# Weight splits handed out earlier in some stretches, and a scan column cleared through its table: a two-layer decoder trunk on one core

## The chip, the cores and the metric

The kernel runs on one core of a Trainium2 chip. The metric is the device time of one execution in microseconds (us), the median over runs. The engines are PE (TensorE: matmuls and transposes), DVE (VectorE), ACT (ScalarE), POOL (GpSimd) and SP (SyncE, which here only issues the loads of weights). Each engine works through its own list of instructions in order; semaphores between the lists keep the data dependences.

## The reference

Two layers on a sequence of 256 positions of width 1024, batch 1, all in float32:

```python
for l in range(DEPTH):                       # DEPTH = 2
    h = h + 0.5 * swiglu(rms_norm(h, ffn1_norm[l]), ...)            # 1024 -> 2816 -> 1024
    h = h + hybrid_mixer(rms_norm(h, mix_norm[l]), w_in[l], ...)    # S5 scan | differential attention
    h = h + memory_cross_attention(rms_norm(h, xattn_norm[l]), rms_norm(mem, mem_norm[l]), ...)
    h = h + 0.5 * swiglu(rms_norm(h, ffn2_norm[l]), ...)
return rms_norm(h, final_norm)
```

The mixer projects its input by `w_in` (1024 to 2048) into the input of a state-space scan (32 groups of 64 complex states, `lax.associative_scan` over the 256 positions) and the q, k, v of a causal differential attention with 4 heads. The scan's result goes through a gelu and a gated projection (`w_glu`, `glu` below). Both halves are normalised, concatenated and projected by `w_out`. The cross-attention reads 256 memory tokens by `wkv` (keys and values).

## The kernel before

*Weights and splits.* All weights are read once, as 512 KB units that SP loads into one of four buffers `raw`. A matmul of float32 accuracy is made of three reduced-precision ones (`fp32r`): a weight is split into a high half `whi` (ACT, with a copy that rounds) and a low half `wlo` (DVE, `raw` less `whi`, scaled by the norm's gain where there is one), the activations into `xh` and `xl` in the same way; PE then does `whi*xh`, `wlo*xh`, `whi*xl`, a triplet of 128x512 matmuls. A unit is split in two steps (q = 0, 1), each one instruction on ACT and one on DVE. Five pairs of `whi` and `wlo` (N_W) are held. In the second feed-forward a unit is split whole, 128x1024 at once. In `wkv` the moving operand is the memory, named `mem`; in the down projections and `w_glu` it is named `gT` or `yT`.

*What sets the order.* The kernel is written out by a planner in Python, which keeps a rough clock for each engine. `stream_plan` (L104) lists all weight units in the order in which PE uses them, and beside it `need`, the planned time of each (2 x STEP = 2.56 units of planned time for an ordinary unit). Before PE's matmuls of a unit are written, `feed` (L503) hands out splits, so that they come next in ACT's and DVE's lists: as long as a buffer is free (N_W) and the split's need is no further off than `LEAD` = 4.0 from where PE's main line is planned to be:

```python
if u >= self.nfree + N_W or (u > least and self.need[u] + q * STEP / 2 > self.main + LEAD):
    break
```

All the other work (evacuation of accumulators, normalisation, softmax, the scan) are tasks, Python generators, which the planner resumes as their planned inputs are due; each resumed step appends its instructions to the engines' lists behind the splits handed out so far. So a longer lead puts more splits ahead of the next step of a task on ACT and DVE, and may change when the planner writes a task's transposes into PE's list. `aside()` writes instructions without advancing the task's planned time.

*First feed-forward (ffn1).* For each of 11 chunks of 256 hidden columns and each half t = 0, 1 of the positions: gate and up matmuls into `mm`; ACT's `sg` (the gate's activation), DVE's `g` (the gated product), PE's transposes `tp<-ident,g`, then `gT` (ACT and DVE); the down matmuls into `acc` follow two chunks later. The second feed-forward (ffn2) has the same steps by way of `z` and combined blocks of weights.

*Mixer.* The projection `w_in` comes in four chunks, then `wkv` in three, so that scan and attention can work meanwhile. The scan's input goes out to DRAM and back (`z` to `uq`), is rearranged by ACT (`up`) and transposed by PE (`tp<-ident,up`) to `U`. 64 small matmuls give the inputs to the states in `acc` (pairs 0, 1 real and 2, 3 imaginary), and DVE then does, for each layer:
- rotations `p<-acc,rot` by a table `rot` (`cs_t` in the code: cosine and sine of each state's phase within a segment of 64 columns, made once in each layer by ACT's Sin),
- two scans `p<-dt,p` over 1023 columns, whose decay table `dt` is zero at the end of each segment,
- rotations back by the same table (`p<-p,rot`, 128x1023), and sums.

Each scan's column 0 of every segment of 64 must be zero: two memsets of 128x16. Attention's scores stand in `sb` (with `bias`), their row maxima in `nm`, the q and k transposes in `qkT`.

*Lines.* In the profile all of DVE's work has line L269, ACT's L306, POOL's L329, PE's matmuls L345 and transposes L356, since helpers record them; tiles are told apart by their names. In the changed kernel these lines are 7 further on.

Of the kernel before, what the change touches and what calls it, by code (L numbers as in the profile page):

```python
# [33 lines left out]
N_W = 5  # L34
N_S4 = 12
N_T5 = 3
LEAD = 4.0
STEP = 1.28
MARGIN = 0.2
BURST = 0.8  # L40
# [63 lines left out]
def stream_plan():  # L104

    plan = []
# [44 lines left out]
    need, at, i = [], 0.0, 0  # L151
    while i < len(plan):
        n = plan[i][5]
        need += [at + STEP * k for k in range(n)]
        at += STEP if plan[i][3] == "S" else 2 * STEP * n
        i += n
    return plan, need


class Task:  # L160


    def __init__(self, gen, now):
        self.gen, self.t, self.done, self.waiters = gen, now, False, []
        self.pe = -1.0
# [195 lines left out]
class Trunk:  # L361
    def __init__(self, ctx, tc, io):
        self.tc, self.io = tc, io
        self.c = Clock(tc.nc)
        self.v, self.a, self.g, self.p = Vector(self.c), Scalar(self.c), Pool(self.c), Tensor(self.c)
        P = lambda name, bufs, **kw: ctx.enter_context(tc.tile_pool(name=name, bufs=bufs, **kw))
        self.const = P("const", 1)
        self.xp = P("xp", 2)
        self.rawp = P("raw", N_RAW)
        self.hip = P("hi", N_W)  # L370
        self.lop = P("lo", N_W)
        self.tab = P("tab", 1)
        self.s4 = P("s4", N_S4)
        self.zp = P("zp", 4)
        self.gp = P("gp", 2)
        self.tp5 = P("tp5", N_T5)
        self.jp = P("jp", 1)
        self.sm = P("sm", 4)
        self.sp1 = P("sp1", 1)
        self.acc = P("acc", 4, space=bass.MemoryType.PSUM)  # L380
        self.mm = P("mm", 2, space=bass.MemoryType.PSUM)
        self.tp = P("tp", 1, space=bass.MemoryType.PSUM)
        self.dram = P("dram", 1, space=bass.MemoryType.DRAM)
        self.plan, self.need = stream_plan()
        self.main = 0.0
        self.upos = self.nload = self.nsplit = self.nfree = 0
        self.raw, self.w, self.blk = {}, {}, {}
        self.added, self.content = set(), {}
        self.stream = Task(None, 0.0)
        self.nacc = self.nmm = 0  # L390
        self.accfree = [0.0, 0.0]
        self.mmfree = [0.0, 0.0]
        self.tpfree, self.tpown = [0.0, 0.0], {}
# [109 lines left out]
    def feed(self, least=-1):  # L503

        c = self.c
        prev, c.cur = c.cur, self.stream
        n = len(self.plan)
        while self.nsplit < 2 * n:
            u, q = divmod(self.nsplit, 2)
            if u >= self.nfree + N_W or (u > least and self.need[u] + q * STEP / 2 > self.main + LEAD):  # L510
                break
            self.split_next(self.plan[u][0].startswith("ffn2"))
        c.cur = prev
# [104 lines left out]
    def tick(self, ready):  # L618
        self.feed()
        self.c.run_due()  # L620
        self.c.now = max(self.c.now, ready + 0.13)
        self.main += STEP / 2

# [57 lines left out]
    def opening(self, evac):  # L681
# [12 lines left out]
        def mm(t, k):  # L694
            u, q = divmod(k, 2)
            self.main += STEP / 2
            self.mm_half(ps[t], self.x[t], self.w[u], 2 * u, q, k == 0, False)
# [21 lines left out]
        self.split_next()  # L719
        self.main += STEP  # L720
        wh, wl = (a[:, 0:512] for a in self.w[0][:2])
# [423 lines left out]
    def ssm_tables(self, l, tb):  # L1145
        v, a, g, io = self.v, self.a, self.g, self.io
# [13 lines left out]
        p = self.sp1.tile([128, 3, 16], F32, tag="sp", name="sp")  # L1160
# [12 lines left out]
        dt, mag, th, n, fr, x1, x2 = (t16(k) for k in ("dt", "mag", "th", "n", "fr", "x1", "x2"))  # L1173
# [24 lines left out]
        cs_t = self.tab.tile([128, 2, 1024], F32, tag="tC", name="rot")  # L1198
# [19 lines left out]
        a.activation(cs, x1, AF.Sin, bias=self.halfpi, scale=-1.0)  # L1218
        a.activation(cs_t[:, 1, :], an, AF.Sin, scale=6.283185)
        a.activation(cs_t[:, 0, :], rn, AF.Sin, bias=self.halfpi, scale=-6.283185)  # L1220
        yield

        pw = self.sp1.tile([128, 2, 16, 5], F32, tag="pw", name="pw")
# [43 lines left out]
        for q in range(4):  # L1267
            yield from self.tp_wait()
            ps = self.tpt()
            for i in range(8):  # L1270
                m, ri = 4 * q + i // 2, i % 2
# [24 lines left out]
        for q in range(2):  # L1296
            yield from self.tp_wait()
            ps = self.tpt()
            for i in range(8):
                m = 8 * q + i  # L1300
                if i == 4:
                    yield self.c.now + GAP
                for e in range(2):
                    s = slice(64 * e, 64 * e + 64)
                    o = ps[64 * e:64 * e + 16, 64 * i:64 * i + 64]
# [23 lines left out]
    def mixer(self, l, preps, tb, tables, tail):  # L1329
        v, c = self.v, self.c  # L1330
# [42 lines left out]
        def ssm_states(z_tasks):  # L1373
# [11 lines left out]
            for b in range(2):  # L1385
                yield from self.tp_wait()
                p = self.transpose4(upf, [512 * b + 128 * k for k in range(4)])
# [5 lines left out]
            for ri in range(2):  # L1393
                for gh in range(2):
                    yield c.now + GAP
                    for pp in range(8):
                        m = 8 * gh + pp
# [24 lines left out]
            n = 1023  # L1422
# [3 lines left out]
            y_r = p2  # L1426
            for o, x in ((y_r, p1), (y_i, p3)):
                v.tensor_tensor_scan(o[:, 1:1024], Dk[:, 0:n], x[:, 0:n], 0.0, ALU.mult, ALU.add)
                v.memset(o.rearrange("p (m c) -> p m c", c=64)[:, :, 0], 0.0)
            yield  # L1430
            xr, xi = p1, y_r
            v.memset(xr[:, 0:1], 0.0)
            s1 = slice(1, 1024)
            tt(xr[:, s1], y_r[:, s1], C[:, 0:n], ALU.mult)
            tt(p3[:, s1], y_i[:, s1], S[:, 0:n], ALU.mult)
# [179 lines left out]
        self.kT = []  # L1615
        zt = self.project("w_in", self.x, ssm_evac, preps)
        states = c.spawn(ssm_states(zt))
        qt = self.project("w_in", self.x, qk_evac(0))
        kt = self.project("w_in", self.x, qk_evac(1))
        vk = []  # L1620
        at = [c.spawn(attn(t, qt + kt, vk)) for t in range(2)]
# [323 lines left out]
```

## Time and profile before

| | |
|---|---|
| median of 3 runs | 1203.88 us (1203.52 to 1204.22) |
| the profiled execution | 1203.8 us |
| its span, first to last instruction | 1201.1 us |
| mean granted clock of PE | 0.998 |
| busy: PE, DVE, ACT, POOL | 1187.6, 903.0, 711.9, 45.3 us |
| mean rate of the HBM | 173 GB/s |

2.7 us of the profiled execution lie around its span. Matmuls are pipelined: a row of PE gives the time of one from its start to its modelled end (0.39 us), while the next one starts 0.23 us after it. "idle before" in square brackets is what an engine stood still ahead of a row, and what ended that.

### The profile page before, as it was taken

How to read it: one execution, taken by the hardware profiler on the slowest of the kernel's cores; microseconds unless marked ns; L12 is line 12 of the kernel's file. 1: busy time of each engine (PE TensorE's matmuls, PEld its weight loads, DVE VectorE, ACT ScalarE, POOL GpSimd, SP SyncE). 2: the span in 40 equal slices, each digit the busy share in tenths (PEclk: the TensorE clock that was granted, in tenths of full speed). 3: DMA queues.
4: the chain of work that ended last, by engine and by line, in shares of the span. 5: the costliest groups of instructions: out<-in, count | busy, mean ns of one | idle time of the engine just before them, and what ended most of it. 6: DMA issues, size and time to landing. Idle time of an engine off the chain costs nothing.

```text
span 1201.1 us, 17736 instructions
## 1 busy us (share of the span) xinstructions
PE 1187.6 (99%) x6583; PEld 971.6 (81%) x6583; DVE 903.0 (75%) x1498; ACT 711.9 (59%) x1206; POOL 45.3 (4%) x104
## 2 busy tenths in 40 slices
PE   9999999999999999999999999999999999999997
PEld 7888888777888888888888888888678888888886
DVE  5797776498866688978668879565978675889785
ACT  6665455556856566555465545555687665666553
POOL 2100001000000000000010000100000000000000
PEclk9999999999999999999999999999999999999999
DMA  8656556534644466374565655654436455746542
GB/s 281 212 182 198 161 172 173 173 124 139 193 159 141 156 219 221 128 263 135 176 194 181 192 171 175 186 168 150 140 121 197 158 158 169 294 133 215 191 140 86
DMA packets 59974, 210.91 MB, mean 176 GB/s; under 512 B 7168, under 2 KB 8288, under 8 KB 59888
## 3 DMA queue, kind: packets, MB, share of 16 engines
q1 hardware_dynamic: 56304, 202.92, 52.5%
q0 software_dynamic: 2000, 5.24, 1.5%
q10 hardware_dynamic: 1584, 1.62, 0.5%
q8 instruction: 51, 0.84, 0.3%
q14 instruction: 35, 0.29, 0.1%
HBM read 207.00 MB, written 1.05 MB: 173 GB/s over the span
## 4 chain that ended last, share of the span: by engine, by line
PE 94%; DVE 2%; DMA 1%; ACT 1%; issue 1%; ACTq 0%; POOLq 0%; POOL 0%; DVEq 0%
PE mm L345 48%; PE acc L345 33%; PE tp L345 8%; PE tp L356 5%; DMA uq<-z 1%; DVE wlo L269 1%; DVE p L269 1%; DMA h<-in_x 0%; ACT whi L306 0%; DVE nm L269 0%; ACT junk L306 0%; ACT z L306 0%; ACT up L306 0%; ACTq L315 0%; PE pz L345 0%
## 5 line engine op out<-in xcount | busy, mean ns | idle before, releaser
L269 DVE SCALAR_TENSOR_TENSOR wlo<-raw,gains,whi 128x512 fp32r<-128x512 f32 x368 | 262.8, 746 | 91.8 <-ACT whi L306 90.3
L345 PE MATMUL mm<-whi,xh 128*128 128x512 f32 x768 | 306.9, 400 | 0.0
L345 PE MATMUL mm<-whi,xl 128*128 128x512 f32 x768 | 300.0, 391 | 0.0
L345 PE MATMUL mm<-wlo,xh 128*128 128x512 f32 x768 | 299.1, 390 | 0.3 <-DVE wlo L269 0.3
L306 ACT ACTIVATE whi<-raw,gains 128x512 fp32r<-128x512 f32 x368 | 240.8, 713 | 12.9 <-issue 5.3
L345 PE MATMUL acc<-whi,gT 128*128 128x512 f32 (+1 forms) x704 | 237.3, 397 | 0.0
L269 DVE TENSOR_TENSOR wlo<-raw,whi 128x512 fp32r<-128x512 f32 (+1 forms) x236 | 209.8, 912 | 20.6 <-ACT whi L306 19.5
L306 ACT ACTIVATE whi<-raw 128x512 fp32r<-128x512 f32 (+1 forms) x236 | 181.4, 806 | 45.0 <-DMA raw<-in_wst 17.3
L345 PEld LDWEIGHTS mm<-whi,xh 128*128 128x128 f32 x768 | 144.5, 188 | 31.6 <-issue 1.3
L345 PEld LDWEIGHTS mm<-whi,xl 128*128 128x128 f32 x768 | 144.3, 188 | 30.6
L345 PEld LDWEIGHTS mm<-wlo,xh 128*128 128x128 f32 x768 | 144.6, 188 | 27.9 <-DVE wlo L269 0.6
L345 PEld LDWEIGHTS acc<-whi,gT 128*128 128x128 f32 x704 | 132.0, 188 | 26.2
L345 PE MATMUL acc<-wlo,gT 128*128 128x512 f32 (+1 forms) x352 | 136.9, 389 | 0.0
L345 PE MATMUL mm<-whi,mem 128*128 128x512 f32 x256 | 92.6, 410 | 0.0
L345 PEld LDWEIGHTS acc<-wlo,gT 128*128 128x128 f32 x352 | 66.3, 188 | 11.6
L306 ACT ACTIVATE sg<-mm,rstd 128x256 f32<-128x256 f32 x44 | 20.9, 475 | 86.5 <-PE mm L345 86.4
L306 ACT ACTIVATE gT<-tp 128x512 fp32r<-128x512 f32 x44 | 26.4, 599 | 55.8 <-PE tp L356 55.8
L306 ACT ACTIVATE z<-mm,rstd 128x256 f32<-128x256 f32 (+1 forms) x52 | 29.7, 572 | 48.8 <-PE mm L345 48.0
L345 PEld LDWEIGHTS mm<-whi,mem 128*128 128x128 f32 x256 | 48.1, 188 | 11.5 <-issue 1.3
L345 PE MATMUL mm<-wlo,mem 128*128 128x512 f32 x128 | 51.0, 398 | 3.8 <-DVE wlo L269 3.8
L306 ACT ACTIVATE xh<-tp 128x512 fp32r<-128x512 f32 x32 | 19.1, 598 | 59.2 <-PE tp L356 59.2
L269 DVE TENSOR_TENSOR gT<-tp,gT 128x512 fp32r<-128x512 f32 x44 | 30.3, 688 | 21.2 <-ACT gT L306 21.2
(261 smaller groups left out, 1546.7 us busy)
## 6 DMA issues: line engine op xcount, KB each, us to landing
raw<-in_wst SPq DMA_DIRECT2D x350, 512.0 KB, 4.1
blkX<-in_wst SPq DMA_DIRECT2D x8, 512.0 KB, 4.7
blkP<-in_wst SPq DMA_DIRECT2D x8, 512.0 KB, 7.8
blkY<-in_wst SPq DMA_DIRECT2D x8, 512.0 KB, 8.7
blkQ<-in_wst SPq DMA_DIRECT2D x8, 512.0 KB, 10.2
raw<-in_wst SPq DMA_DIRECT2D x4, 256.0 KB, 5.7
mem<-in_mem POOLq DMA_DIRECT2D x2, 512.0 KB, 7.1
uq<-z ACTq DMA_DIRECT2D x8, 128.0 KB, 4.5
```

What stands on the lines that cost most here:

```text
L269: r = getattr(self.e, name)(*a, **k)
L306: r = self.e.activation(out, in_, func, **k)
L345: r = self.e.matmul(out, lhsT, rhs, **k)
L356: r = self.e.transpose(out, in_, ident)
```

## The change

Two things are changed.

1. Column 63 of each segment of the table `rot` (cosine and sine) is set to zero by POOL, once in each layer, after ACT's Sin. The product that the last column of a segment contributes to the scan, and the one that it contributes to the first column of the next segment behind it, are thereby zero, and the two memsets of a scan's columns on DVE are left out. One memset of 128x1 (`xi[:,0:1]`) comes in for the column that no scan writes.
2. `stream_plan` gives a lead for each unit, and `feed` uses it. It is 6.0 instead of 4.0 for the units of ffn1 and ffn2 from the 17th of the stage on (but for the last ones, whose matmuls are taken four units at a time), of `w_in` from the fifth on, and of `wkv`'s first eight.

```diff
+LEAD_LONG = 6.0
...
-    return plan, need
+    ahead, at, stage = [], 0, None
+    for nm, l, n, kind, _, skew in plan:
+        at = at + 1 if (nm[:4], l) == stage else 0
+        stage = nm[:4], l
+        long = nm[:3] == "ffn" and at >= 16 and skew == 1 or nm == "w_in" and at >= 4 or nm == "wkv" and n < 8
+        ahead.append(LEAD_LONG if long else LEAD)
+    return plan, need, ahead
...
-        self.plan, self.need = stream_plan()
+        self.plan, self.need, self.ahead = stream_plan()
...
-            if u >= self.nfree + N_W or (u > least and self.need[u] + q * STEP / 2 > self.main + LEAD):
+            if u >= self.nfree + N_W or (u > least and self.need[u] + q * STEP / 2 > self.main + self.ahead[u]):
...
         a.activation(cs_t[:, 0, :], rn, AF.Sin, bias=self.halfpi, scale=-6.283185)
+        with self.c.aside():
+            g.memset(cs_t.rearrange("p r (m c) -> p r m c", c=64)[:, :, :, 63:64], 0.0)
         yield
...
                 v.tensor_tensor_scan(o[:, 1:1024], Dk[:, 0:n], x[:, 0:n], 0.0, ALU.mult, ALU.add)
-                v.memset(o.rearrange("p (m c) -> p m c", c=64)[:, :, 0], 0.0)
             yield
             xr, xi = p1, y_r
             v.memset(xr[:, 0:1], 0.0)
+            v.memset(xi[:, 0:1], 0.0)
```

What it moves in the engines' lists. In the rows below a number behind a tile's name only tells one buffer's use from another; a split's `raw` number is that of its unit.

*Mixer, layer 0: PE's list where the transposes of `up` stand.* Before:

```order
L345 MATMUL mm_2303<-whi_2310,xh_2197 128x512
L345 MATMUL mm_2303<-wlo_2311,xh_2197 128x512
L345 MATMUL mm_2303<-whi_2310,xl_2198 128x512
L345 MATMUL mm_2303<-whi_2310,xh_2197 128x512
L345 MATMUL mm_2303<-wlo_2311,xh_2197 128x512
L345 MATMUL mm_2303<-whi_2310,xl_2198 128x512
L356 MATMUL tp_2367<-ident_125,up_2354 128x128 x4
L356 MATMUL tp_2373<-ident_125,up_2354 128x128 x4
L345 MATMUL mm_2302<-whi_2330,xh_2125 128x512
```

and in the changed kernel, where `whi_2296` is what `whi_2310` was before and `whi_2322` what `whi_2330` was:

```order
L352 MATMUL mm_2307<-whi_2322,xh_2122 128x512
L352 MATMUL mm_2307<-wlo_2323,xh_2122 128x512
L352 MATMUL mm_2307<-whi_2322,xl_2123 128x512
L352 MATMUL mm_2307<-whi_2322,xh_2122 128x512
L352 MATMUL mm_2307<-wlo_2323,xh_2122 128x512
L352 MATMUL mm_2307<-whi_2322,xl_2123 128x512
L363 MATMUL tp_2382<-ident_125,up_2366 128x128 x4
L363 MATMUL tp_2388<-ident_125,up_2366 128x128 x4
L352 MATMUL mm_2308<-whi_2322,xh_2198 128x512
```

The transposes have moved by six matmuls, behind the first half of the next unit.

*The same place on ACT.* From `up` on, before:

```order
L306 ACTIVATE up_2354<-uq_2253 128x4x16x16
L306 ACTIVATE whi_2350<-raw_2273,gains_107 128x512
L306 ACTIVATE U_2366<-tp_2367 128x512
L306 ACTIVATE U_2366<-tp_2373 128x512
L306 ACTIVATE whi_2385<-raw_2293,gains_107 128x512
L306 ACTIVATE z_2394<-mm_2302,rstd_2159 128x512
L306 ACTIVATE whi_2385<-raw_2293,gains_107 128x512
L306 ACTIVATE qkT_2393<-tp_2422 128x4x128
L306 ACTIVATE z_2444<-mm_2303,rstd_2245 128x512
L306 ACTIVATE whi_2470<-raw_2319,gains_107 128x512
L306 ACTIVATE qkT_2393<-tp_2474 128x4x128
L306 ACTIVATE whi_2470<-raw_2319,gains_107 128x512
```

and now:

```order
L313 ACTIVATE up_2366<-uq_2262 128x4x16x16
L313 ACTIVATE whi_2362<-raw_2285,gains_107 128x512
L313 ACTIVATE U_2381<-tp_2382 128x512
L313 ACTIVATE U_2381<-tp_2388 128x512
L313 ACTIVATE whi_2397<-raw_2311,gains_107 128x512
L313 ACTIVATE z_2402<-mm_2307,rstd_2160 128x512
L313 ACTIVATE z_2411<-mm_2308,rstd_2250 128x512
L313 ACTIVATE whi_2397<-raw_2311,gains_107 128x512
L313 ACTIVATE qkT_2401<-tp_2435 128x4x128
L313 ACTIVATE qkT_2401<-tp_2463 128x4x128
L313 ACTIVATE whi_2488<-raw_2331,gains_107 128x512 x2
```

The units that are `whi_2350`, `whi_2385` and `whi_2470` before are `whi_2342`, `whi_2362` and `whi_2397` now, and `whi_2488` is the next one (before `whi_2519`). Before, the last row but one is a `qkT` and half of the unit `whi_2470` stands behind it; now that unit stands ahead of both `qkT`, whole, and the next one follows.

*DVE, the start of the rotations in layer 0.* Before:

```order
L269 SCALAR_TENSOR_TENSOR wlo_2386<-raw_2293,gains_107,whi_2385 128x512 x2
L269 SCALAR_TENSOR_TENSOR wlo_2471<-raw_2319,gains_107,whi_2470 128x512 x2
L269 TENSOR_TENSOR p_2503<-acc_2389,rot_884 128x512
L269 TENSOR_TENSOR p_2503<-acc_2390,rot_884 128x512
L269 TENSOR_TENSOR p_2504<-acc_2391,rot_884 128x512
L269 TENSOR_TENSOR p_2504<-acc_2392,rot_884 128x512
```

and now:

```order
L276 SCALAR_TENSOR_TENSOR wlo_2398<-raw_2311,gains_107,whi_2397 128x512 x2
L276 SCALAR_TENSOR_TENSOR wlo_2489<-raw_2331,gains_107,whi_2488 128x512 x2
L276 TENSOR_TENSOR p_2515<-acc_2407,rot_899 128x512
L276 TENSOR_TENSOR p_2515<-acc_2408,rot_899 128x512
L276 TENSOR_TENSOR p_2516<-acc_2409,rot_899 128x512
L276 TENSOR_TENSOR p_2516<-acc_2410,rot_899 128x512
```

The last split ahead of the rotations is that of `whi_2470`'s unit before, and that of the unit behind it now.

*DVE, the scans in layer 0* (the rows `p<-dt,p`; the profile calls them TENSOR_TENSOR_SCAN). Before:

```order
L269 SCALAR_TENSOR_TENSOR wlo_2639<-raw_2528,gains_107,whi_2638 128x512
L269 SCALAR_TENSOR_TENSOR p_2504<-dt_885,p_2503 128x1023
L269 MEMSET p_2504 128x16
L269 SCALAR_TENSOR_TENSOR p_2578<-dt_885,p_2505 128x1023
L269 MEMSET p_2578 128x16
L269 SCALAR_TENSOR_TENSOR sb_2629<-acc_2623,bias_136 128x256
L269 SCALAR_TENSOR_TENSOR sb_2629<-acc_2624,bias_136 128x256
L269 SCALAR_TENSOR_TENSOR wlo_2639<-raw_2528,gains_107,whi_2638 128x512
L269 SCALAR_TENSOR_TENSOR sb_2650<-acc_2631,bias_136 128x512
L269 SCALAR_TENSOR_TENSOR sb_2650<-acc_2632,bias_136 128x512
L269 SCALAR_TENSOR_TENSOR wlo_2670<-raw_2551,gains_107,whi_2669 128x512
L269 MEMSET p_2503 128x1
```

and now:

```order
L276 SCALAR_TENSOR_TENSOR wlo_2612<-raw_2513,gains_107,whi_2611 128x512
L276 SCALAR_TENSOR_TENSOR p_2516<-dt_900,p_2515 128x1023
L276 SCALAR_TENSOR_TENSOR p_2573<-dt_900,p_2517 128x1023
L276 SCALAR_TENSOR_TENSOR wlo_2612<-raw_2513,gains_107,whi_2611 128x512
L276 SCALAR_TENSOR_TENSOR sb_2640<-acc_2634,bias_136 128x256
L276 SCALAR_TENSOR_TENSOR sb_2640<-acc_2635,bias_136 128x256
L276 SCALAR_TENSOR_TENSOR wlo_2658<-raw_2540,gains_107,whi_2657 128x512
L276 SCALAR_TENSOR_TENSOR sb_2653<-acc_2642,bias_136 128x512
L276 SCALAR_TENSOR_TENSOR sb_2653<-acc_2643,bias_136 128x512
L276 MEMSET p_2515 128x1
L276 MEMSET p_2516 128x1
```

The 128x16 memsets are gone, the split's second half has moved from behind two `sb` to right behind the scans, and a memset of 128x1 has come in.

*A chunk of ffn1 in layer 1, DVE.* `g_7167` and `g_7186` are the products of the two halves t, before:

```order
L269 SCALAR_TENSOR_TENSOR W_6969<-W_6969,Wt_6970 128x16x16
L269 SCALAR_TENSOR_TENSOR g_7167<-mm_7082,rstd_5766,sg_7166 128x256
L269 TENSOR_TENSOR wlo_7161<-raw_7077,whi_7160 128x512
L269 TENSOR_TENSOR W_6969<-bc_5957,pw_6492 128x16x16 x2
L269 SCALAR_TENSOR_TENSOR g_7186<-mm_7083,rstd_5852,sg_7185 128x256
L269 SCALAR_TENSOR_TENSOR wlo_7196<-raw_7101,gains_107,whi_7195 128x512
L269 TENSOR_TENSOR Wt_6970<-bc_5957,pw_6492 128x256 x2
L269 SCALAR_TENSOR_TENSOR wlo_7196<-raw_7101,gains_107,whi_7195 128x512
L269 TENSOR_TENSOR gT_7210<-tp_7182,gT_7210 128x512
```

and now (`g_7164`, `g_7187`):

```order
L276 SCALAR_TENSOR_TENSOR g_7164<-mm_7079,rstd_5766,sg_7163 128x256
L276 SCALAR_TENSOR_TENSOR wlo_7171<-raw_7083,gains_107,whi_7170 128x512
L276 TENSOR_TENSOR W_7063<-W_7063,Wt_7064 128x16x16
L276 SCALAR_TENSOR_TENSOR W_7063<-W_7063,Wt_7064 128x16x16
L276 SCALAR_TENSOR_TENSOR wlo_7171<-raw_7083,gains_107,whi_7170 128x512
L276 SCALAR_TENSOR_TENSOR g_7187<-mm_7080,rstd_5852,sg_7186 128x256
L276 TENSOR_TENSOR W_7063<-bc_5957,pw_6510 128x16x16 x2
L276 SCALAR_TENSOR_TENSOR wlo_7202<-raw_7105,gains_107,whi_7201 128x512 x2
L276 TENSOR_TENSOR gT_7214<-tp_7179,gT_7214 128x512
```

Two splits of one unit (`wlo_7171`) stand between the two `g` now, where one stood. In PE's list there are 9 matmuls between the transposes of these two `g` before, and 12 now.

## The prediction

> **What bounds the kernel now.** I read the page's first part and its chain first: who is busy, and what the end hangs on.
>
> ```profile
> PE 1187.6 (99%) x6583; PEld 971.6 (81%) x6583; DVE 903.0 (75%) x1498; ACT 711.9 (59%) x1206; POOL 45.3 (4%) x104
> ...
> PE 94%; DVE 2%; DMA 1%; ACT 1%; issue 1%; ACTq 0%; POOLq 0%; POOL 0%; DVEq 0%
> ```
>
> TensorE (PE) is busy for 1187.6 of 1201.1 us, and 94% of the chain is PE. The change takes no big matmul away, so it can win only what PE idles: 1201.1 - 1187.6 = 13.5 us. The waits of PE say which part is within reach:
>
> ```profile
> PE mm L345 <- DVE wlo L269: 4.1, 5, 1.4
> PE pz L345 <- DVE zero L269: 1.2, 1, 1.2
> PE tp L356 <- ACT up L306: 0.7, 2, 0.5
> ...
> PE mm L345 <- DVE wlo L269: 2.0, 2, 1.4
> ...
> PE mm L345 <- DVE wlo L269: 1.9, 2, 1.3
> ```
>
> (Columns: us in total, times, longest.) The first three rows are the whole span, the fourth is its stretch 255 to 275 us (layer 0), the fifth 850 to 870 us (layer 1). So 3.9 of 4.1 us stand at one place in each layer: the first units of the memory's key and value weights, wkv, where PE waits for VectorE's low halves (wlo). The other place is the transposes of `up`. PE's timeline at both in layer 0:
>
> ```profile
> 227.95 0.39 PE L345 MATMUL mm<-whi,xl 128*128 128x512 f32 x1
> 228.82 0.88 PE L356 MATMUL tp<-ident,up 128*128 128x128 f32 x6 [0.48 <-ACT up L306]
> ...
> 263.12 0.39 PE L345 MATMUL mm<-wlo,xh 128*128 128x512 f32 x1
> ...
> 264.03 0.62 PE L345 MATMUL mm<-whi,mem 128*128 128x512 f32 x2
> 266.06 0.50 PE L345 MATMUL mm<-wlo,mem 128*128 128x512 f32 x1 [1.41 <-DVE wlo L269]
> 266.40 0.63 PE L345 MATMUL mm<-whi,mem 128*128 128x512 f32 x2
> ...
> 268.49 0.63 PE L345 MATMUL mm<-whi,mem 128*128 128x512 f32 x2
> 269.11 0.51 PE L345 MATMUL mm<-wlo,mem 128*128 128x512 f32 x1
> ...
> 271.52 0.62 PE L345 MATMUL mm<-whi,mem 128*128 128x512 f32 x2
> 272.70 0.50 PE L345 MATMUL mm<-wlo,mem 128*128 128x512 f32 x1 [0.56 <-DVE wlo L269]
> ```
>
> Matmuls overlap, so their cost is read from start to start. Undisturbed it is 0.227 us for one (263.12 to 264.03 are four). Why wlo is late is seen on VectorE (DVE) and ScalarE (ACT):
>
> ```profile
> 234.44 0.60 ACT L306 ACTIVATE qkT<-tp 128x512 f32<-128x512 f32 x1 [1.81 <-PE tp L356]
> ...
> 238.83 0.60 ACT L306 ACTIVATE qkT<-tp 128x512 f32<-128x512 f32 x1 [2.60 <-PE tp L356]
> 239.33 3.78 ACT L306 ACTIVATE whi<-raw,gains 128x512 fp32r<-128x512 f32 x6
> ...
> 240.07 0.75 DVE L269 SCALAR_TENSOR_TENSOR wlo<-raw,gains,whi 128x512 fp32r<-128x512 f32 x1 [3.06 <-ACT whi L306]
> 240.74 2.48 DVE L269 TENSOR_TENSOR p<-acc,rot 128x512 f32<-128x512 f32 x4
> ...
> 254.74 4.61 DVE L269 TENSOR_TENSOR_SCAN p<-dt,p 128x1023 f32<-128x1023 f32 x2
> 257.11 2.40 DVE L269 MEMSET p<- 128x16 f32 x2
> 259.80 0.75 DVE L269 SCALAR_TENSOR_TENSOR sb<-acc,bias 128x256 f32<-128x256 f32 x2 [0.29 <-issue]
> ...
> 265.27 0.74 DVE L269 SCALAR_TENSOR_TENSOR wlo<-raw,gains,whi 128x512 fp32r<-128x512 f32 x1
> ...
> 267.19 1.21 DVE L269 TENSOR_REDUCE nm<-sb 128x4 f32<-128x1024 f32 x1
> 268.31 1.40 DVE L269 SCALAR_TENSOR_TENSOR wlo<-raw,gains,whi 128x512 fp32r<-128x512 f32 x2
> 269.64 1.22 DVE L269 TENSOR_TENSOR p<-p,rot 128x1023 f32<-128x1023 f32 x1
> 270.77 1.22 DVE L269 TENSOR_TENSOR p<-p 128x1023 f32<-128x1023 f32 x1
> 271.91 1.41 DVE L269 SCALAR_TENSOR_TENSOR wlo<-raw,gains,whi 128x512 fp32r<-128x512 f32 x2
> ```
>
> ACT stands idle for 1.81 and 2.60 us, waiting at the head of its line for a transpose while splits could run; DVE waits 3.06 us for it and then hardly stops from 240 to 272, with the state-space work (rotations, two scans) and the splits in one line. The wlo of 265.27, 268.31 and 271.91 are the three that PE waits for. A backlog that begins with idle time just ahead of it is what an earlier hand-out mends.
>
> **The change part by part.**
>
> *wkv.* What PE loses in layer 0, by start to start: 264.03 to 266.06 should be 2 x 0.227 = 0.45 and is 2.03, so 1.58; 268.49 to 269.11 is 0.62, so 0.17; 271.52 to 272.70 is 1.18, so 0.73. The matmul behind each also starts 0.34 after it (266.06 to 266.40, 269.11 to 269.45) in place of 0.23: 0.11 x 3 = 0.33. Together 2.8 us; layer 1, whose wait row is 0.1 shorter, 2.7.
>
> Does it go? The chain gives PE's side:
>
> ```profile
> 221.60 6.00 DMA uq<-z
> ...
> 238.80 1.08 PE acc L345 x32
> ```
>
> One piece of the state-space accumulation takes 1.08, and the last ends at 239.88. With lead 6, one unit (two splits) more stands ahead of the rotations in DVE's order, and in PE's order the second qk transposes stand ahead of the third piece instead of behind it: with the 0.55 that `up` no longer loses (below) and some 0.15 for more changes between kinds of matmul, 1.08 + 0.55 - 0.15 = 1.5 sooner. ACT then copies them at 237.35 instead of 238.83, and 0.5 later (238.83 to 239.33) begins the two splits at 0.61 each (3.78 less 0.7, over 5): they end at 238.55 and 239.2. DVE's two wlo, at 0.66 (1.40 - 0.74), follow: the rotations begin at 239.9, not at 240.74, with 1.32 us less behind them. So DVE is 0.85 + 1.3 = 2.15 us ahead at the scans (252.6). Behind them the cleared columns fall away: 2 x 0.07 less 0.06, and most of the 0.29 of issue, 0.3 in all. Against the use by PE, which comes 0.55 sooner for `up`:
> - The first late wlo ended at 266.01; now 266.01 - 2.45 = 263.55. PE uses it at 264.03 + 0.45 - 0.55 = 263.95. Margin 0.4.
> - The second ended at 269.05; now 2.45 sooner, and a reduction (267.19 to 268.31, 1.1) stands behind it in the new order: 265.5. Use: 268.49 + 0.45 - 0.55 - 1.58 - 0.11 = 266.7. Margin 1.2.
> - The third ended at 272.65; now two products (269.64 to 271.91, 2.3) stand behind it: 267.9. Use: 271.52 + 0.45 - 0.55 - 1.69 - 0.28 = 269.45. Margin 1.5.
>
> So I take 5.5 gained in both layers. Bounds: 5.5, and 1.0 if DVE gains the 0.3 at the scans alone and the two later waits 0.1 each (0.5 in each layer).
>
> *up.* 227.95 + 0.227 = 228.18, and the transposes start at 228.82: 0.64, of which some 0.1 belongs to the change from one kind of matmul to the other. What is awaited is the transfer of `uq` above: it lands at 227.60 whatever DVE does. The transposes now stand six matmuls (1.36 us) later in PE's order, at 229.6, and `up` ended at 228.77: the stall of 0.55 goes. In layer 1 the wait is shorter (0.7 in all, 0.5 in layer 0): 0.3. Together 0.85; bounds 0 and 1.0.
>
> *The cleared columns.* DVE loses two 128x16 memsets for one of 128x1 in each layer, and POOL gains one of 128x32:
>
> ```profile
> L269 DVE MEMSET p<- x6: 59/72/72, 257.1 to 854.9; 128x16 f32 x4, 128x1 f32 x2
> ...
> 615.23 0.18 POOL L329 MEMSET pw<- 128x16 f32 x2
> ```
>
> On DVE 2 x 0.072 - 0.059 = 0.09 us and up to 0.3 of issue: counted above, worth nothing to PE by itself with a backlog of 1.6. On POOL two of 128x16 take 0.18, so one of 128x32 about 0.2; it waits for ACT's sines, and behind it stand the two pw memsets and the transfers of `ks`, which come from later work of ACT (POOL is 4% busy). If that cover were gone it costs 0.2 us twice. I count 0.
>
> *The longer lead in the feed-forward stages.* No wait of wlo is seen there worth the name (0.2 us of 4.1), so there is nothing to win and only something to lose: a split more stands ahead of each evacuation (sg, g, and the transposes of g on PE) on ACT and DVE.
>
> ```profile
> 742.85 0.47 ACT L306 ACTIVATE sg<-mm,rstd 128x256 f32<-128x256 f32 x1 [5.10 <-PE mm L345]
> ...
> 743.36 0.48 DVE L269 SCALAR_TENSOR_TENSOR g<-mm,rstd,sg 128x256 f32<-128x256 f32 x1 [1.50 <-ACT sg L306]
> ...
> 744.01 0.38 PE L356 MATMUL tp<-ident,g 128*128 128x128 f32 x2
> ...
> 745.16 0.48 DVE L269 SCALAR_TENSOR_TENSOR g<-mm,rstd,sg 128x256 f32<-128x256 f32 x1
> ...
> 746.32 0.38 PE L356 MATMUL tp<-ident,g 128*128 128x128 f32 x2
> ```
>
> The first g ends at 743.84, 0.17 before its use; the second at 745.64, 0.68 before. First ones stay as they are: no split is put between the last matmul and sg. For the second, at this place, ACT now does two splits between the sg: 743.22 + 2 x 0.61 = 744.44, so sg is 0.23 later; DVE does a wlo more (0.66), g ends at about 746.35. The transposes now come twelve matmuls after the first instead of nine: 746.32 + 0.68 = 747.0. Margin 0.65, so it is covered. Where the order gives less cover I allow a tenth of a us here and there: 0.5 us lost in all; bounds 0 and 3 (the 44 groups of g that the page counts, at 0.07).
>
> [...]
>
> *Sum.* 5.5 + 0.85 - 0.5 = 5.85 us off the profiled execution's 1203.8, which stands 0.1 below the median of the runs: 1198.0 against 1203.88. A measurement here tells some 0.2%, 2.4 us, from nothing.
>
> **The rivals.**
>
> 1. *The wait moves on.* The splits and the scans are no less work, only earlier, and N_W holds five units; a backlog may come back at the gated projection (w_glu), whose splits stand among yT and on. For it: DVE is 75% busy over the whole, and its hump is long. Against: DVE's lead of 2.45 us reaches into this stretch. If one wait like the longest (1.58 + 0.11) comes in each layer: 1198.0 + 3.4 = 1201.4.
>
> 2. *The wait stays.* If the rotations wait for the accumulation rather than for the splits, DVE gains only the 0.3 behind the scans, and the bound of 1.0 holds: 1203.8 - 1.0 - 0.85 + 0.5 = 1202.5. For it: the accumulation ends at 239.88, as late as my new start of the rotations. Against: only the last two of the four rotations need its last pieces, and the unit split ahead of them is off DVE's line in any case.
>
> 3. *Slower: the evacuations stand behind the longer line.* Of the 44 g, 22 are second ones. If each is one wlo (0.66) later than its cover, 0.68 less the shift where PE's order has none, up to 0.5 us is lost in each: 22 x 0.5 = 11, and 1203.8 - 6.35 + 11 = 1208.5. It decides from a mean of 0.29 us on (6.35 over 22). Against: the place above, where the shift covers it.
>
> **How the numbers follow.** My forecast 0.63; its own range is 1197.0 (nothing lost: 1197.5, and half a us for waits too short to be listed) to 1200.5 (the 3 us bound). Rival 1: 0.15. Rival 2: 0.10. Rival 3: 0.12. Range: 1196.8 to 1203.0 leaves out rival 3 and a little below. Faster by over 0.2% (below 1201.5): the forecast, and most of rival 1, 0.74. Within 0.2%: the rest of rival 1 and rival 2, 0.15. Slower: the greater part of rival 3, 0.11.
>
> **What the profile after would show.** Right: the rows of PE waiting for wlo and `up` fall from 4.1 and 0.7 us to under 0.5 together; the scans start some 2.5 us sooner relative to PE's work; DVE's 3.06 us idle shrinks; PE's busy time stays at 1187 to 1188. Wrong: a new row of PE waiting for DVE g, gT or ACT z in the feed-forward stages (rival 3), a wlo row with w_glu's matmuls (rival 1), or the wkv row at over 2 us (rival 2).

## The result and the profile after

The changed kernel takes 1196.71 us (median of 4 runs, 1196.30 to 1196.96), the kernel before beside it 1204.05 (4 runs, 1203.52 to 1204.32): 7.3 us less, a ratio of 0.9939 (95% interval 0.9922 to 0.9956). The forecast was 5.85 us less. The profiled execution took 1196.59 us, its span 1194.8. From the page, busy times and the chain of waits:

```profile
PE 1185.4 (99%) x6583; PEld 970.2 (81%) x6583; DVE 901.6 (75%) x1496; ACT 710.4 (59%) x1206; POOL 46.8 (4%) x106
...
PE 98%; ACT 1%; DMA 0%; issue 0%; DVE 0%; POOLq 0%; POOL 0%; ACTq 0%; DVEq 0%
```

The chain is 98% PE, where it was 94%: DVE and the transfer of `uq` have left it. What PE waited for over the whole span (us in total, times, longest):

```profile
PE pz L352 <- DVE zero L276: 1.2, 1, 1.2
PE mm L352 <- ACT whi L313: 0.7, 1, 0.7
PE tp L363 <- DMA h<-in_x: 0.3, 1, 0.3
PE mm L352 <- DVE wlo L276: 0.3, 1, 0.3
```

All four lie in the first 9 us. The waits for wlo at wkv (3.9 us) and for `up` (0.7) are gone from both layers. PE's timeline shows it at the transposes of `up`, which start 0.23 us behind the matmul ahead of them (228.84 to 229.07), as that one does behind the one before it:

```profile
228.84 0.39 PE L352 MATMUL mm<-whi,xl 128*128 128x512 f32 x1
229.07 1.04 PE L363 MATMUL tp<-ident,up 128*128 128x128 f32 x8
...
262.59 0.39 PE L352 MATMUL mm<-wlo,mem 128*128 128x512 f32 x1
...
263.28 0.39 PE L352 MATMUL mm<-wlo,mem 128*128 128x512 f32 x1
```

The row of 263.28 is the matmul that came 1.58 us late before; it now starts three matmuls (0.69 us) behind the one of 262.59. On DVE:

```profile
237.54 1.41 DVE L276 SCALAR_TENSOR_TENSOR wlo<-raw,gains,whi 128x512 fp32r<-128x512 f32 x2 [3.58 <-ACT whi L313]
238.87 2.48 DVE L276 TENSOR_TENSOR p<-acc,rot 128x512 f32<-128x512 f32 x4
...
250.67 1.41 DVE L276 SCALAR_TENSOR_TENSOR wlo<-raw,gains,whi 128x512 fp32r<-128x512 f32 x2 [1.23 <-ACT whi L313]
252.00 4.46 DVE L276 TENSOR_TENSOR_SCAN p<-dt,p 128x1023 f32<-128x1023 f32 x2
...
261.84 0.74 DVE L276 SCALAR_TENSOR_TENSOR wlo<-raw,gains,whi 128x512 fp32r<-128x512 f32 x1
...
263.10 1.41 DVE L276 SCALAR_TENSOR_TENSOR wlo<-raw,gains,whi 128x512 fp32r<-128x512 f32 x2
```

The whole execution starts its big matmuls 0.57 us sooner (7.97 before, 7.40 now, read from PE's timeline), so 0.57 has to be added to compare. The rotations begin at 238.87 + 0.57 = 239.4 instead of 240.74, the scans at 252.6 instead of 254.74, and the split that was late first before now ends at 261.84 + 0.74 = 262.58, 0.7 ahead of its use at 263.28.

Two of the signs that the prediction named came out otherwise: DVE's idle time ahead of the rotations has grown, from 3.06 to 3.58 us, and PE's busy time fell to 1185.4 us.

### The profile page after: what moved, and what is told of

Same layout as the page of the kernel before. It is cut to its first block, busy times and chain, and to the rows that moved or that the text cites. A ratio compares the mean times of both kernels' runs of the same rounds, so it can differ in the third digit from the quotient of the medians.

```text
span 1194.8 us, 17732 instructions
## 1 busy us (share of the span) xinstructions
PE 1185.4 (99%) x6583; PEld 970.2 (81%) x6583; DVE 901.6 (75%) x1496; ACT 710.4 (59%) x1206; POOL 46.8 (4%) x106
## 4 chain that ended last, share of the span: by engine, by line
PE 98%; ACT 1%; DMA 0%; issue 0%; DVE 0%; POOLq 0%; POOL 0%; ACTq 0%; DVEq 0%
PE mm L352 52%; PE acc L352 33%; PE tp L352 8%; PE tp L363 5%; DMA gains<-in_gains 0%; ACT junk L313 0%; ACT whi L313 0%; DVE h L276 0%; ACT z L313 0%; ACT on L313 0%; DVE wlo L276 0%; POOLq L1950 0%; ACT xh L313 0%; POOL rstd L336 0%; DVE fo L276 0%
## 5 line engine op out<-in xcount | busy, mean ns | idle before, releaser
L276 DVE SCALAR_TENSOR_TENSOR g<-mm,rstd,sg 128x256 f32<-128x256 f32 x44 | 21.2, 482 | 42.7 <-ACT sg L313 42.7
```

The costliest lines, as they stand in the source:

```text
L276: r = getattr(self.e, name)(*a, **k)
```

## The experiments

Each kernel was timed in turn with the kernel before, whose median beside them was 1203.96 to 1204.44 us.

### Before, again, and each part alone

**again**: the kernel before, unchanged.

> The kernel before, unchanged, beside itself. The changed kernel's profile has 5.8 us less of PE waiting behind the opening, but its time is 7.3 us lower; 0.57 us of the rest lies ahead of PE's first big matmul (7.97 us after the span's start before, 7.40 now) and 0.9 outside the span (2.7 us around it before, 1.8 now). Theory A, these two belong to the program and repeat: every run of the kernel before has about 2.7 us around its span, a span within 1200.5 to 1201.5, and a ratio of 1.000. Rival, they are chance of the one profiled execution: here the time around the span or the first matmul comes out near 1.8 and 7.4 in some runs, and the time then is 1 to 1.5 us lower.

1204.03 us, ratio 0.9999 (0.9990 to 1.0008). The profiled execution took 1203.31 with a span of 1201.5: 1.8 us around it, not 2.7. PE's first big matmul starts at 7.61, not 7.97. Its wait for `up`:

```profile
PE tp L356 <- ACT up L306: 1.4, 2, 0.7
```

So 2.7 around the span and the late opening were a draw of that one execution, as the rival had it, but the time is no lower than that of the others: the wait for `up` was 1.4 here and 0.7 there. All executions of the kernel before with a recorded span, 92 in this section, say the same. Their span has a median of 1202.1 us (1200.9 to 1204.0), 1.0 above that of the execution from which the forecast was made, and only 17 of them have more than 2.2 us around it.

**clear_only**: the first part of the change.

```diff
-        long = nm[:3] == "ffn" and at >= 16 and skew == 1 or nm == "w_in" and at >= 4 or nm == "wkv" and n < 8
+        long = False
```

> Only the first part of the change: the table's column cleared by POOL, the scans' memsets gone, all leads 4. My theory: DVE is 0.3 us further behind each pair of scans at the least, so the first wkv wait shrinks from 1.58 to about 1.2 in each layer and the others by 0.1: 0.6 to 1.2 us faster (1202.7 to 1203.3). Rival (the clearing carries the gain, since it also moves the planner's clock): 3 us or more faster.

1209.99 us, ratio 1.0055 (1.0043 to 1.0068): 5.6 slower, which neither theory had. Its waits of PE:

```profile
PE tp L352 <- DVE yT L276: 5.4, 2, 2.7
PE mm L352 <- DVE wlo L276: 2.9, 5, 0.7
PE tp L363 <- ACT up L313: 1.2, 2, 0.8
```

The wkv wait shrinks, from 4.1 to 2.9, but a new one of 2.7 us comes in each layer: the planner, whose clock of DVE has two memsets less, writes the steps behind the scan in another order. PE and ACT there:

```profile
293.42 0.60 PE L363 MATMUL tp<-ident,yg 128*128 128x128 f32 x4
...
294.55 0.60 PE L363 MATMUL tp<-ident,yg 128*128 128x128 f32 x4
...
298.55 1.86 PE L352 MATMUL tp<-z,aT 128*128 128x128 f32 x7 [2.70 <-DVE yT L276]
```

```profile
292.44 1.28 ACT L313 ACT_TABLE_LOAD   x1
293.74 0.51 ACT L313 ACTIVATE sb<-sb,nm 128x256 f32<-128x256 f32 x1
...
295.72 0.71 ACT L313 ACTIVATE whi<-raw,gains 128x512 fp32r<-128x512 f32 x1
296.33 1.06 ACT L313 ACTIVATE yT<-tp 128x512 fp32r<-128x512 f32 x1
```

Both transposes of `yg` stand close together and fill the two `tp` buffers; the copies that free them (yT) stand on ACT behind a table load, four exponentials of the second softmax and a split, so the attention's next product, which needs a `tp` buffer, holds PE up. The waiting is not all of the loss: from 298.0 to 301.4 us, and again from 895.3 to 898.7 behind the wait in layer 1, PE's granted clock is 0.50 (what that costs is seen in w_in_only below). In the kernel before and in the changed one the softmax is done ahead of `yg`, and the two transposes stand further apart.

**clear_same_order**: the same clearing, but the planner still reckons with the memsets.

```diff
                 v.tensor_tensor_scan(o[:, 1:1024], Dk[:, 0:n], x[:, 0:n], 0.0, ALU.mult, ALU.add)
+                self.c.engine("dve", 16 * 0.3e-3 + 0.07)
...
-            v.memset(xi[:, 0:1], 0.0)
+            with self.c.aside():
+                v.memset(xi[:, 0:1], 0.0)
```

> Clearing the table as in the change, all leads 4, but the planner still reckons with the two memsets that DVE no longer does, so that PE's and ACT's lists are those of the kernel before, word for word, and DVE's too but for the memsets. Clearing with its own order was 5.5 us slower, with a new wait of PE for DVE's yT, 2.7 us in each layer. Theory: that loss is the order alone, and the instructions themselves are worth what the first wkv wait loses: 0.6 to 1.2 us faster than before. Rival: the clearing costs by itself (POOL's memset, or the table's zeros): 1 us or more slower.

1202.77 us, ratio 0.9991 (0.9982 to 0.9999), 1.4 less than before (0.1 to 2.2 by the interval). Its waits:

```profile
PE mm L352 <- DVE wlo L276: 2.8, 5, 0.7
PE tp L363 <- ACT up L313: 1.7, 2, 1.2
```

The first wkv wait falls from 1.4 to 0.7 in each layer. DVE's rows show the 0.7:

```profile
254.45 4.46 DVE L276 TENSOR_TENSOR_SCAN p<-dt,p 128x1023 f32<-128x1023 f32 x2
258.82 0.73 DVE L276 SCALAR_TENSOR_TENSOR sb<-acc,bias 128x256 f32<-128x256 f32 x2
```

From the start of the scans to the `sb` behind them it takes 258.82 - 254.45 = 4.37 us; with the memsets, in the kernel before, it took 259.80 - 254.74 = 5.06. So two memsets whose rows are 0.07 us long hold DVE up by 0.69: 0.15 within the two scans, 0.29 idle ahead of `sb`, the rest at the second memset. The instructions of the clearing are thus worth 1.4 us on the kernel before, and the order that they bring about costs 7.0 (5.6 and 1.4): two waits of 2.7 us and the two stretches of half clock behind them.

**lead_only**: the second part alone, the two memsets kept on DVE. Its lists on PE and ACT are those of the changed kernel, word for word.

> Only the second part: lead 6 in the named stretches, the scans' memsets kept on DVE. My theory: the three wkv waits and the wait for up go as in the whole change, at most 0.2 us of the first wait comes back in each layer (its margin was reckoned at 0.4, of which 0.3 is the memsets'): 6.5 to 7.3 us faster, 1196.7 to 1197.5. Rival: without the clearing the first wait comes back by 0.4 or more in each layer, 1198 or later.

1196.83 us, ratio 0.9944 (0.9930 to 0.9957): all of the change's gain. With the longer lead the clearing is worth nothing that can be measured. DVE's list differs by more than the memsets: the split that ends at 262.58 in the changed kernel stands further ahead here and ends at 260.34, 2.7 ahead of its use.

### Which stretch of the lead

**mixer_only**: the change without the feed-forward stretches.

```diff
+        long = nm == "w_in" and at >= 4 or nm == "wkv" and n < 8
```

> Clearing and lead 6 in w_in and wkv alone; the feed-forward stages keep lead 4. My theory: all of the gain is made in the mixer, and the longer lead in the feed-forward stages costs 0.2 to 0.4 us (PE falls back by 0.2 in ffn1 of layer 1 in the trace): 1196.2 to 1196.8, the same as the whole change or up to 0.5 faster. Rival: the feed-forward lead brings 0.5 us or more, 1197.3 or later.

1196.86 us, ratio 0.9943 (0.9931 to 0.9956), the same as the whole change.

**ffn_only**: the feed-forward stretches alone, no clearing.

```diff
+        long = nm[:3] == "ffn" and at >= 16 and skew == 1
```

> Lead 6 in the feed-forward stages alone, no clearing. Theory: nothing to win there, 0 to 0.4 us slower; PE's waits in the mixer as before (wlo 3.9 us, up 0.7 to 1.4 us). The waits for up are a transfer's and differ from execution to execution, which is where the 1.5 us that the forecast lacked would come from: the kernel before has 0.7 us of them in one profile and 1.4 in another. Rival: the missing 1.5 us are the feed-forward lead's, which shows here as 1 us or more faster.

1204.32 us, ratio 1.0000 (0.9991 to 1.0008). In its profile the transfer of `uq` takes 7.12 us (chain of waits), where it took 6.00 before, and PE waits for `up` accordingly, 1.6 us in layer 0; its waits, then the chain:

```profile
PE tp L363 <- ACT up L313: 2.0, 2, 1.6
```

```profile
221.51 7.12 DMA uq<-z
```

**w_in_only** and **wkv_only**: one of the mixer's two stretches, no clearing.

```diff
+        long = nm == "w_in" and at >= 4        # w_in_only
+        long = nm == "wkv" and n < 8           # wkv_only
```

> Lead 6 in w_in from its fifth unit alone, no clearing. Theory: the unit that moves ahead of the rotations belongs to w_in, so the wait for up goes and the wkv waits mostly (first 0 to 0.6 in each layer); what comes back later is open, since wkv's lead of 4 lets the backlog of splits build up behind: 4 to 7 us faster. Rival: wkv's own lead is what takes its waits away; then the wkv wait stays at 1.5 to 2 us in each layer and only up goes, 1 to 2 us faster.

> Lead 6 in wkv's first eight units alone, no clearing. Theory: nothing moves ahead of the rotations, up waits as before, and DVE is as far behind at the scans, so the first wkv waits stay: 0 to 2 us faster. Rival, as above: wkv's waits go, 4.5 us or more faster.

1206.73 us, ratio 1.0024 (1.0015 to 1.0033), and 1205.38, ratio 1.0011 (1.0002 to 1.0020): each alone is slower (wkv_only only just, by its interval), while together, in lead_only and mixer_only, they are 7.6 faster. In w_in_only `up` is gone and the wkv waits have shrunk; in wkv_only the wkv waits are under 0.9 and `up` is as before. Both fell where clear_only fell:

```profile
PE tp L352 <- DVE yT L276: 5.4, 2, 2.7
PE mm L352 <- DVE wlo L276: 1.9, 6, 0.5
```

```profile
PE tp L352 <- DVE yT L276: 4.1, 2, 2.1
PE tp L363 <- ACT up L313: 1.6, 2, 1.0
...
PE mm L352 <- DVE wlo L276: 0.9, 3, 0.3
```

(w_in_only, then wkv_only.) In wkv_only the two transposes of `yg` stand side by side in PE's list. What each stretch wins is as the first theory had it for `w_in`, and as the rival had it for `wkv`; both missed the yT wait that decides the time.

w_in_only also shows what the clock costs. The wait is 2.72 us in both layers, but only the one in layer 1 is followed by a stretch of half clock. The eight transposes behind it, and the windows from there on (busy time of PE, PEld, DVE, ACT and POOL, granted clock PEclk, DMA share, GB/s), layer 0 and layer 1:

```profile
296.82 1.16 PE L352 MATMUL tp<-z,aT 128*128 128x128 f32 x8 [2.72 <-DVE yT L276]
890.06 2.08 PE L352 MATMUL tp<-z,aT 128*128 128x128 f32 x8 [2.72 <-DVE yT L276]
```

```profile
296.80:300.20 3.40, 3.38 (x19) 2.77 (x19) 3.26 (x8) 2.37 (x10) 0.00 (x0) 1.00 0.50 142
890.00:893.40 3.40, 3.34 (x12) 3.06 (x13) 3.26 (x9) 1.50 (x5) 0.00 (x0) 0.50 0.50 137
```

At half clock PE runs 12 matmuls in the window in which it runs 19 at full clock, and it is 0.9 to 1.6 us behind when the same matmuls of the two layers are compared, here and in wkv_only. In the profiles such a stretch stands at the end of the span, where PE's work is over; otherwise it follows four of the six waits of 2.0 us or more (two of two in clear_only, one of two in each of w_in_only and wkv_only) and none of the shorter ones, up to 1.6 us. What decides between the two layers is not shown.

**lead5_mixer** and **lead8_mixer**: mixer_only with LEAD_LONG = 5.0 and 8.0.

> Clearing and lead 5 in place of 6 in w_in and wkv; feed-forward lead 4. The splits are handed out half a unit sooner: both of the unit at the rotations stand ahead of the second qk transposes on ACT, but no unit more ahead of the rotations on DVE, and the transposes of yg stand as before (not close together). Theory: DVE's rotations begin about 0.9 us sooner and the scans' clearing adds 0.3, so the first wkv wait falls from 1.58 to 0.3 to 0.6 and the later two go; up loses one triplet's worth: 4.5 to 6 us faster than before, 1198.3 to 1199.7. Rival: only a whole unit more mends the wait: 2 us faster or less.

> Clearing and lead 8 in w_in and wkv, feed-forward lead 4. The transposes of yg stand 18 matmuls apart, the second attention product behind them. Theory: nothing is left to win, since PE waits for nothing in the mixer with lead 6; five pairs of buffers cap the lead: within 0.5 us of the changed kernel, if the order brings no new wait. Rival: evacuations now stand behind more splits, 1 us or more slower than lead 6.

1199.89 us, ratio 0.9965 (0.9951 to 0.9979), and 1200.94, ratio 0.9975 (0.9967 to 0.9984). Their waits, 5 and then 8:

```profile
PE mm L352 <- DVE wlo L276: 1.3, 3, 0.5
...
PE tp L363 <- ACT up L313: 1.1, 2, 0.7
```

```profile
PE acc L352 <- DVE wlo L276: 2.1, 4, 0.9
...
PE mm L352 <- ACT z L313: 0.5, 2, 0.3
PE tp L363 <- ACT U L313: 0.5, 2, 0.3
```

Lead 5 does about half, just under the theory's gain. Lead 8 brings the rivals that 6 escapes: evacuations (z, U) late behind splits, and a wait for wlo at matmuls into `acc` (2.1 us), the longest, 0.9, at `acc<-wlo,xh` at 329.35 us and again at 920.61 in layer 1.

### DVE's lateness and `up`, one at a time

**slack_probe** and **slack_scans**: the changed kernel with one product of 128x1024 more on DVE in each layer, ahead of the rotations or ahead of the scans.

```diff
+            self.v.e.tensor_tensor(p1, C, S, op=ALU.mult)      # slack_probe, ahead of rot(p1, R, C)
...
+            self.v.e.tensor_tensor(y_r, C, S, op=ALU.mult)     # slack_scans, ahead of the scans
```

> The whole change, and ahead of the first rotation in each layer DVE does one product of 128x1024 more (1.15 us by the trace), which nobody needs and which the planner isn't told of: PE's list is that of the changed kernel, word for word. In the changed kernel's trace the wlo of the first late wkv split ends 0.7 us before PE uses it, those behind it 0.9 to 1.8, and two at w_glu 0.06 and 0.26. Theory: about 0.5 us comes back at the first wkv wait in each layer, 0.1 to 0.4 at others: 1.0 to 2.0 us slower than the changed kernel, 1197.7 to 1198.8. Rivals: DVE's place in this stretch doesn't matter (the order of PE's list alone made the gain): within 0.4 us of the changed kernel. Or the margins are used up all along the stretch: 3 us or more slower.

> The whole change, with one product of 128x1024 more on DVE (1.15 us) right ahead of the scans in each layer, which nobody needs; PE's list is that of the changed kernel, word for word. The same product ahead of the rotations cost nothing (1196.58): DVE has an idle 1.23 us behind them, ahead of the scans, waiting for ACT. Here nothing lies between it and the first late wkv split, whose wlo ends 0.7 us before its use, and the third, at 0.9 (unit 85). Theory: 0.45 us of wait for the first split and 0.1 for one switch of PE in each layer, up to 0.3 for unit 85: 1.0 to 1.7 us slower than the changed kernel, 1197.6 to 1198.3. Rival: DVE's place doesn't matter, within 0.4 of 1196.6.

For slack_probe 1196.58 us, ratio 0.9938 (0.9926 to 0.9951): nothing lost, where the theory had 1.0 to 2.0 us. DVE's rows of slack_probe show why:

```profile
238.92 1.22 DVE L1422 TENSOR_TENSOR p<-rot 128x1024 f32<-128x1024 f32 x1
240.24 2.49 DVE L276 TENSOR_TENSOR p<-acc,rot 128x512 f32<-128x512 f32 x4
...
250.08 2.07 DVE L276 SCALAR_TENSOR_TENSOR wlo<-raw,gains,whi 128x512 fp32r<-128x512 f32 x3
252.07 4.46 DVE L276 TENSOR_TENSOR_SCAN p<-dt,p 128x1023 f32<-128x1023 f32 x2
```

The rotations are 1.37 later, the scans only 0.07: the 1.23 us that DVE stood idle at 250.67 have been used up. With the product behind that idle time, in slack_scans, 1198.35 us, ratio 0.9949 (0.9936 to 0.9961), 1.6 to 1.8 slower than the changed kernel, and PE waits again at the same split (layer 0):

```profile
263.90 0.51 PE L352 MATMUL mm<-wlo,mem 128*128 128x512 f32 x1 [0.44 <-DVE wlo L276]
```

So the wkv wait is DVE's lateness at the scans, with about 0.7 us to spare, and not PE's order.

**up_later**: the kernel before with `up` and its transposes one triplet later on PE, by a planned time of the transfer's task 1.0 longer; all DVE rows as before.

```diff
                 self.a.dma_start(st["uq"][r0:r0 + 32], z[:, gh * 256:gh * 256 + 256])
+            c.cur.t += 1.0
```

> The kernel before, but the transposes of up stand one triplet (3 matmuls, 0.68 us) later in PE's list in both layers and the copy of up one split later in ACT's; all other rows as before. Seven profiles without the longer w_in lead show 0.7, 1.2, 1.4, 1.6, 1.7 and 2.0 us of waiting for up in all, 0.7 in the one that the forecast was made from. Theory: that was a low draw, a usual execution loses 1.4 or more there, and 1.0 to 1.4 us go: 1202.8 to 1203.4 beside 1204.2. Rival: the wait of 0.7 is the usual one: 0.4 to 0.7 us faster. Rival: the time that PE gains there is lost at the wkv wait, since DVE's work is no sooner: 0 to 0.3 faster.

1202.26 us, ratio 0.9989 (0.9980 to 0.9998): 1.7 less. What is left in its profile, where PE waits for wlo as long as before:

```profile
PE mm L345 <- DVE wlo L269: 4.2, 5, 1.4
...
PE tp L356 <- ACT up L306: 0.7, 2, 0.4
```

**up_and_clear**: up_later and clear_same_order together.

> The kernel before with the transposes of up one triplet later (measured alone: 1.7 us faster) and the table cleared instead of the scans' columns, in the order of before (alone: 1.2 us faster). Leads all 4. Theory: the terms stand side by side; the clearing shortens the first wkv wait from 1.4 to 0.7 in each layer whatever up does, since PE and DVE are both sooner: 2.4 to 3.2 us faster than before, 1200.9 to 1201.7. Rival: PE, sooner by up, runs into the wkv wait, since DVE isn't sooner: 1.2 to 1.8 us faster, and up's price is partly what the wkv wait would have cost.

1200.93 us, ratio 0.9973 (0.9962 to 0.9983): 3.2 less, where 1.7 and 1.4 make 3.1. Within the intervals the terms add.

No version tried is faster than the changed kernel by more than runs differ; lead_only, mixer_only and it are one time.

## Why the prediction was right and wrong

*The waits.* Right: both places that it named, and no other wait of PE behind the opening has gone. Read from PE's progress (the start of the same big matmul in both traces), the mixer's stretch with `up` brings 0.78 us in layer 0 and 0.53 in layer 1, wkv and what follows 2.5 and 2.3, and the feed-forward stages cost 0.3: 5.8 us behind the opening, where the sum had 5.85. That these two agree is in part luck: `up` brought 1.3 against 0.85 in this pair of executions, wkv 4.8 against 5.5. And the pair differs by 7.2 us, for 0.57 lies in the opening and 0.9 around the span, which the sum put at nothing.

*`up`, the term that was mis-sized.* The step that failed is the sum's 0.85 us for `up`, with an upper bound of 1.0, read from one execution, in which the transfer of `uq` took 6.00 us. The wait is a draw: in the kernels with the old w_in lead it came to 0.7, 1.4, 1.2, 1.7, 2.0 and 1.6 us in six profiles. Read start to start, from the matmul ahead of the transposes to the one behind them, which takes 1.02 us in each layer of the changed kernel, these six lose 1.2, 1.8, 1.6, 2.2, 2.5 and 2.1 us in both layers together, 1.9 in the mean. So the forecast's own execution held 1.2, the lowest of the six: the 0.1 that was taken off for a change between kinds of matmul does not exist there, as the transposes now start 0.23 us behind the matmul ahead (ahead of the small matmuls `acc<-U,VT` it does: 0.33 us, from 231.10 to 231.43 in the changed kernel), and the 0.3 for layer 1 was low. Moving the transposes by one triplet, which can win 1.36 us in both layers together, won 1.7 (0.2 to 2.4 by the interval) and left 0.7 of waiting in its profile. A usual execution thus loses about 2 us there, twice the bound.

The forecast's execution nevertheless had a usual time, because it also had 0.9 us more around its span and an opening 0.2 to 0.9 later than in the others: a low `up` and a high rest that cancelled. The change takes `up` away and leaves the rest. That is some 1.0 to 1.2 us (1.9 to 2, less 0.85) of the 1.3 by which the time came out under the forecast, and puts it 0.09 us below the range. The bounds of this term came from the one execution too, and so did the lower end.

The account does not close. With 1.9 for `up`, 4.8 for wkv and 0.3 lost in the feed-forward stages the terms make 6.4, and the opening is 0.2 later with the old w_in lead than with the longer one, in the mean of eight profiles each (7.6 and 7.4), which makes 6.6 of the 7.3 that the medians differ by. The remaining 0.7 is within the interval of the measurement (5.3 to 9.4 us), but no profile shows where it lies; both profiles of the kernel before were of executions below the median.

*wkv.* The margins were reckoned well: 0.4, 1.2 and 1.5 us, and 0.7, 1.5 and 1.8 by the trace. One step in it was wrong without harm: the rotations do begin sooner, and the scans begin at 252.6 as forecast, but slack_probe shows that their start isn't what carries the gain. DVE waits for ACT again before the scans; what counts is that less work stands behind that wait (two splits, 1.33 us from 250.67 to 252.00). Before, 254.74 - 249.63 = 5.1 us of work stood behind the last such wait (DVE's timeline of the kernel before):

```profile
249.63 0.75 DVE L269 SCALAR_TENSOR_TENSOR wlo<-raw,gains,whi 128x512 fp32r<-128x512 f32 x1 [0.77 <-ACT whi L306]
```

That 252.6 was met is in part luck, for the forecast had added the gain at the rotations to that behind them. Of the 5.5 forecast 4.8 came. 0.3 in each layer is given back at w_glu, where a wlo ends just as PE wants it and the matmul starts 0.4 behind the one ahead instead of 0.23, and the next one 0.34:

```profile
314.87 0.61 PE L352 MATMUL acc<-whi,yT 128*128 128x512 f32 x2
315.49 0.50 PE L352 MATMUL acc<-wlo,yT 128*128 128x512 f32 x1
315.83 0.63 PE L352 MATMUL acc<-whi,yT 128*128 128x512 f32 x2
```

That is the first rival's place (the wait moves on to w_glu), at about a sixth of its price (0.3 where it had 1.69 in each layer).

*The cleared columns.* Counted 0 for POOL and 0.3 a layer for DVE. It is 0.69 in layer 0 by clear_same_order, more than twice as much, and as much as the 0.7 to spare at the first late split. What the forecast did not see is that an edit which takes two memsets of about 0.07 us from the planner's clock can bring an order that costs 7.0, so that the clearing by itself is 5.6 slower. The diff's two parts had to be read together.

*The feed-forward lead.* 0.5 lost by forecast, none that can be measured (ffn_only 1.0000, mixer_only as the whole), 0.3 in the trace. The third rival is out: at the place shown in the forecast the second g ends 0.56 us ahead of its transposes, which was put at 0.65:

```profile
742.43 0.48 DVE L276 SCALAR_TENSOR_TENSOR g<-mm,rstd,sg 128x256 f32<-128x256 f32 x1
```

```profile
743.47 0.38 PE L363 MATMUL tp<-ident,g 128*128 128x128 f32 x2
```

What standing behind other work costs shows in the runs elsewhere: in clear_only the first yT copy begins at 296.33, 2.3 us after the first four transposes of `yg` have ended (293.42 + 0.60 = 294.02), with exponentials and a split ahead of it in ACT's list, and in lead8_mixer PE waits for z and U by up to 0.3 us at a time.

## What to carry to other kernels

A wait of PE for DVE or ACT that has an idle stretch of that engine just ahead of it can be mended by handing work out sooner, as the 3.9 us of waits for wlo at wkv were here; look for the last idle stretch in front of it, since here time won or lost ahead of that did not reach PE (slack_probe: 1.37 us lost at the rotations, 0.07 of it left at the scans). Where a sum is made against one profiled execution, a term that is a transfer's length needs several executions, and the rest of that execution (opening, time around the span) has to be usual as well. Where a planner sets the order, every small edit is a draw of a new order: compare it in the old order as well, and look at its waits, and at the granted clock behind them, before keeping or dropping it.

## What had not been expected of the hardware

The way of z out to DRAM and back as `uq` (128 KB transfers) took 6.00 us on the chain in one profile (the kernel before) and 7.12 in another (ffn_only). The time around the span was 1.7 to 2.2 us in 167 of the 194 executions in the experiments' lists, of old and new kernels alike, and 2.2 to 3.2 in the other 27. Behind four of six waits of PE of 2.0 to 2.7 us its granted clock fell to 0.50 for 3.4 us (clear_only, w_in_only, wkv_only), which cost 0.9 to 1.6 us more. A product of 128x1024 on DVE, 1.22 us by its row, cost nothing ahead of the rotations (slack_probe) and 0.8 to 0.9 us in each layer ahead of the scans (slack_scans), though DVE is busy 75% of the time over the whole. Two memsets with rows of 0.07 us, beside scans on DVE, held it up by 0.69 us in layer 0 and 0.66 in layer 1 (from the scans' start to the row behind them 5.06 and 5.03 us before, and 4.37 without the memsets: clear_same_order in layer 0, the changed kernel in layer 1), and 1.4 us came when they were taken away.
